# Two transformer blocks with 64 experts on one core: other first experts, bias tables without GpSimd, a shorter seam, shared products split

## The chip, the cores and the metric

The kernel runs on one core of a Trainium2 chip. The metric is the device time of one execution in microseconds; three executions of the kernel before were timed. A fourth was taken by the hardware profiler, and every row below is from that one. TensorE (PE) multiplies; VectorE (DVE), ScalarE (ACT) and GpSimd (POOL) work elementwise; SyncE (SP) issues nearly all DMAs, each in the order of its queue.

## The reference

The input is one sequence of 256 tokens, 1024 wide. The first block has two layers. Each adds a mixture of three branches (windowed attention with a bias by relative position, a convolution over 31 positions, latent attention) and a feed-forward of 4096. After a final norm the second block modulates the rows with a vector, runs retention and a gated delta rule, and then 64 experts: each token goes to 8 of them, out of 4 of 8 groups, beside one expert that all tokens share. Everything is float32.

```python
def swa_bias_and_mask(positions, rel_bias):
    ...
    bucket = t5_bucket(pq[..., :, None] - pk[..., None, :])
    bias = rel_bias[bucket].astype(jnp.float32).reshape(b, nb, WINDOW, 2 * WINDOW, SWA_KV_HEADS, SWA_GROUP)
...
def first_block(x, positions, rel_bias, g_final, ...):
    swa_bias, swa_mask = swa_bias_and_mask(positions, rel_bias)
    for l in range(DEPTH):
        h = rms_norm(x, g_mix[l])
        q_a, k_a, v_a, u_b, cq_c, ckv_c, kpe_c, gate_logits = jnp.split(h @ w_in[l], IN_SPLIT_POINTS, axis=-1)
        y_a = swa_attention(q_a, k_a, v_a, swa_sinks[l], swa_bias, swa_mask)
        y_b = conformer_conv(u_b, w_dw[l], b_dw[l], g_conv_ln[l], b_conv_ln[l])
        y_c = mla_attention(cq_c, ckv_c, kpe_c, positions, ...)
        branches = jnp.einsum('bsnc,ncd->bsnd', jnp.stack([y_a, y_b, y_c], axis=2), w_branch[l])
        gates = jax.nn.sigmoid(gate_logits.reshape(b, s, N_BRANCHES, D_MODEL))
        x = x + jnp.einsum('bsnd,bsnd->bsd', gates, branches) @ w_out[l]
        h = rms_norm(x, g_mlp[l])
        x = x + jnp.square(jax.nn.relu(h @ w_up[l])) @ w_down[l]
    return rms_norm(x, g_final)
...
def _moe(h, w_router_l, bias_l, w_gate_l, w_up_l, w_down_l, w_sh_gate_l, w_sh_up_l, w_sh_down_l):
    scores = jax.nn.sigmoid((xt @ w_router_l).astype(jnp.float32))
    ...
    sel = lax.top_k(cand, TOP_K)[1]
    wts = jnp.take_along_axis(scores, sel, axis=1)
    wts = wts / jnp.sum(wts, axis=-1, keepdims=True) * ROUTED_SCALE
    ...
        return (jax.nn.silu(xe @ w_gate_l[e]) * (xe @ w_up_l[e])) @ w_down_l[e]
    ...
    shared = (jax.nn.silu(xt @ w_sh_gate_l) * (xt @ w_sh_up_l)) @ w_sh_down_l
    return (routed + shared).reshape(b, l, d)
```

## The kernel before

Activations lie transposed, model dimension on partitions, 256 tokens along the free axis. Dense weights are read as 128 x 1024 tiles of 512 KB (`raw`, line 323). ScalarE rounds each to a high part `whi`, VectorE (some GpSimd) subtracts it and keeps the low part `wlo`; a dense product is three products of 256 tokens, X high and low with `whi` and X high with `wlo`. `Kern.run` goes through layer 0 (`mix`, `ff`), layer 1, the final norm, the mixers of the second block (`mixer2`) and the experts (`moe`). Except for the experts' part, a scheduler sets each engine's order.

*Bias tables.* `t5_bias` (line 423) builds `self.bias`, the position bias of both windows for eight heads, in layer 0. Six times GpSimd subtracts positions of 16 keys from those of 128 queries into `n` (int32, 128 x 2048, two buffers), VectorE compares `n` with a threshold on each partition into `oh` (bf16, two buffers), TensorE multiplies `oh` with three parts of the bias differences, and VectorE adds the mask, head by head: 48 additions of 128 x 64. Queries, keys, values and the convolution's gate `gt` are projected at the same time; their `wlo` splits are in the same VectorE queue.

*Seam.* The last feed-forward's output comes in pairs of tiles: `bt` is the product scaled, `xT` the sum with the residual. `add_sq` (line 506) squares each tile on ScalarE (`sq`, once plain, once with the final gain) and sums them on GpSimd (`sqacc`). `final_norm` (line 1346) sums over partitions on TensorE, takes an inverse root on VectorE (`rsqrt`, line 470), spreads it over all partitions (`rows`, line 489), and then does the same for the norm that follows in the second block; `modulated` (line 928) makes the eight tiles of the input `X` with it, and `final_x` (beside it in the queue) the normed residual `xT`.

*Experts.* Weights of this stage go through `ring` (line 1618), 25 slots of 512 KB in which a tile is loaded once and read as it is. SP issues them in the order of the code. The shared expert has four tiles `w_sh` and two `w_shd`; each expert six, four `w_gu` (gate and up) and two `w_ed` (down). Experts are sorted by their number of tokens on the device. The tables `TIERS` give the positions in that order (first position, token slots for each expert), and `ORDER` the sequence of groups; a group has 256 slots and two units of 128 slots, so a unit holds one, two or four experts. The first `PRE` of the sorted experts are fixed, 0, 1 and 2 here, whatever their counts: their tiles are issued without knowing the routing. For the others SP loads the expert's number (`ids`) first, and so waits for the router. 

```python
NRING = 25
PRE = 3
TIERS = ((0, 128), (8, 64), (32, 32))
ORDER = (0, 2, 0, 1, 1, 2, 0, 1, 1, 2, 0, 1, 1, 2)
...
        j = U["js"][i]
        if j < PRE:
            return slice(j, j + 1)
        if i not in U["reg"]:
            U["reg"][i] = self.nc.values_load(self.ids[0:1, j:j + 1], engines=[mybir.EngineType.SP], ...
```

With these tables the first group holds experts 0 and 1, 128 slots each. `shared` (line 1771) multiplies all four `w_sh` tiles ahead of the experts (`st` is its activation, `hs` its hidden rows). `experts` (line 1834) writes TensorE's order by hand: `gather` makes a one-hot matrix `oh` on VectorE and copies the group's tokens with products `pm<-oh,tok` into `xg`; a unit then has `gate_up` (line 1888, `pd<-ring,xg`), the next group's gathering, and `down` (`pm<-ring,hT`). `overflow` (line 1973) is a branch on the device: if any expert has more tokens than its tier has slots (counts against the tiers, `fl`), it reads the experts again.

## Time and profile before

| | us |
|---|---|
| median of three executions | 1885.78 (1885.19 to 1888.55) |
| profiled execution, whole | 1888.56 |
| its span | 1886.8 |
| PE busy | 1769.1 (94%) |
| DVE busy | 1203.6 (64%) |
| ACT busy | 780.9 (41%) |
| POOL busy | 212.5 (11%) |
| bytes by DMA | 414.45 MB, 220 GB/s over the span |

The busy time of an engine is an average over stages that differ. The first block lasts to about 1050 us, the mixers to about 1340, the experts to the end. In the last row, the mean of 220 GB/s stands for slices of 81 to 251 GB/s up to about 1415 us and of 406 to 409 behind that, but for the last.

### The profile page before, as it was taken

Reading aid. Unit: us, or ns where it says so; the run is one execution under the profiler, and the core shown is the slowest. Engines: PE = TensorE matmul, PEld = TensorE weight load, DVE = VectorE, ACT = ScalarE, POOL = GpSimd, SP = SyncE. Lnnn points to the kernel's source line nnn. Section 1 sums busy time; section 2 is a strip of 40 time slices with the busy share of each in tenths; the row PEclk is TensorE's granted clock in tenths of the full one; section 3 lists DMA queues with packets and bytes.
Section 4 is the critical chain, followed back from the end, with each engine's and each line's share of the span. In section 5 each row is a group of like instructions: output and inputs, shape, how many; then the busy total and the mean of one; then the engine's idle time right before and its main releaser. Section 6 shows DMA issues by size and latency. Waiting matters only on the chain.

```text
span 1886.8 us, 37800 instructions
## 1 busy us (share of the span) xinstructions
PE 1769.1 (94%) x15105; PEld 1462.3 (78%) x15105; DVE 1203.6 (64%) x2383; ACT 780.9 (41%) x1409; POOL 212.5 (11%) x158
## 2 busy tenths in 40 slices
PE   5988999999999999999999899899999999999996
PEld 5987999999997899999889798799854443443441
DVE  7989887988798687866857688458622332332323
ACT  4247655444447655555354445444322121221211
POOL 3344200000053502000002000000100000000000
PEclk9889999999999999999989899999899999999999
DMA  4334555777542456756545342334579999999996
GB/s 158 118 101 127 176 168 178 251 240 247 170 138 81 158 168 201 225 172 199 160 146 178 95 145 81 110 102 131 211 250 398 408 408 409 409 409 409 408 406 237
DMA packets 122146, 414.45 MB, mean 220 GB/s; under 512 B 13937, under 2 KB 14833, under 8 KB 121969
## 3 DMA queue, kind: packets, MB, share of 16 engines
q1 hardware_dynamic: 120528, 409.92, 61.9%
q8 instruction: 119, 1.95, 0.4%
q10 hardware_dynamic: 1440, 2.11, 0.4%
q14 instruction: 59, 0.48, 0.1%
HBM read 410.92 MB, written 1.05 MB: 218 GB/s over the span
## 4 chain that ended last, share of the span: by engine, by line
PE 51%; DMA 13%; DVE 4%; issue 3%; ACT 2%; POOL 2%; SPq 0%; POOLq 0%; DVEq 0%; ACTq 0%
PE pd L290 36%; PE pm L290 14%; DMA ring<-in_w_gu 8%; DMA ring<-in_w_ed 4%; POOL wlo L302 1%; PE pst L290 1%; PE pm L966 1%; POOL sqacc L302 1%; DVE wlo L302 1%; DVE iY L302 0%; ACT iZ L299 0%; ACT whi L299 0%; ACT E L299 0%; PE pm L1926 0%; DVE pst L311 0%
## 5 line engine op out<-in xcount | busy, mean ns | idle before, releaser
L290 PE MATMUL pd<-X,whi 128*128 128x256 f32 (+1 forms) x3280 | 635.8, 294 | 11.9 <-ACT whi L299 8.3
L299 ACT ACTIVATE whi<-raw 128x1024 fp32r<-128x1024 f32 x340 | 356.8, 1052 | 504.2 <-PE pd L290 393.1
L290 PEld LDWEIGHTS pd<-X,whi 128*128 128x128 f32 (+1 forms) x3280 | 532.6, 198 | 17.0 <-ACT whi L299 8.5
L290 PE MATMUL pd<-X,wlo 128*128 128x256 f32 (+1 forms) x1640 | 481.0, 294 | 15.3 <-DVE wlo L302 12.1
L302 DVE TENSOR_TENSOR wlo<-raw,whi 128x1024 fp32r<-128x1024 f32 x286 | 352.9, 1238 | 115.2 <-ACT whi L299 114.1
L290 PEld LDWEIGHTS pd<-X,wlo 128*128 128x128 f32 (+1 forms) x1640 | 324.7, 198 | 19.9 <-DVE wlo L302 13.4
L290 PE MATMUL pd<-ring,xg 128*32 128x512 f32 (+2 forms) x1024 | 235.2, 596 | 10.0 <-DMA ring<-in_w_gu 9.9
L290 PEld LDWEIGHTS pd<-ring,xg 128*32 128x32 f32 (+2 forms) x1024 | 71.6, 130 | 168.6 <-issue 108.8
L290 PE MATMUL pd<-H,whi 128*128 128x256 f32 x1024 | 185.5, 283 | 0.0
L290 PEld LDWEIGHTS pd<-H,whi 128*128 128x128 f32 x1024 | 157.6, 189 | 0.5
L311 DVE SCALAR_TENSOR_TENSOR tg<-tg,pd 128x256 f32<-128x256 f32 x28 | 11.8, 421 | 219.4 <-ACT tg L299 219.4
L302 POOL TENSOR_TENSOR wlo<-raw,whi 128x1024 fp32r<-128x1024 f32 (+1 forms) x54 | 127.5, 2373 | 170.4 <-ACT whi L299 155.2
L290 PE MATMUL pd<-H,wlo 128*128 128x256 f32 x512 | 143.9, 281 | 0.0
L311 DVE SCALAR_TENSOR_TENSOR pst<-up,vec,pst 128x256 f32<-128x256 f32 x240 | 116.4, 485 | 3.7
L290 PE MATMUL pm<-ring,hT 128*32 128x512 f32 (+2 forms) x512 | 111.4, 598 | 2.7 <-DMA ring<-in_w_ed 1.7
L299 ACT ACTIVATE tg<-pd 128x256 f32<-128x256 f32 x28 | 10.8, 384 | 235.4 <-PE pd L290 235.4
L311 DVE SCALAR_TENSOR_TENSOR acc<-rawm,sl,acc 128x512 f32<-128x512 f32 x112 | 87.6, 794 | 20.8 <-DMA rawm<-in_w_mod 20.3
L290 PEld LDWEIGHTS pd<-H,wlo 128*128 128x128 f32 x512 | 96.5, 189 | 0.0
L302 DVE TENSOR_TENSOR y<-pm,y 128x512 fp32r<-128x512 f32 x56 | 38.5, 691 | 86.8 <-ACT y L299 86.8
L302 POOL TENSOR_TENSOR sqacc<-sqacc,sq 128x256 f32<-128x256 f32 x42 | 37.3, 897 | 488.4 <-ACT sq L299 487.2
L299 ACT ACTIVATE y<-pm 128x512 fp32r<-128x512 f32 (+1 forms) x58 | 34.4, 597 | 121.8 <-PE pm L290 121.8
L290 PEld LDWEIGHTS pm<-ring,hT 128*32 128x32 f32 (+2 forms) x512 | 33.3, 129 | 65.9 <-issue 52.4
(532 smaller groups left out, 2645.0 us busy)
## 6 DMA issues: line engine op xcount, KB each, us to landing
ring<-in_w_gu SPq DMA_DIRECT2D x256, 512.0 KB, 10.1
ring<-in_w_ed SPq DMA_DIRECT2D x128, 512.0 KB, 10.1
raw<-in_w_up SPq DMA_DIRECT2D x64, 512.0 KB, 4.2
raw<-in_w_dn SPq DMA_DIRECT2D x64, 512.0 KB, 4.2
raw<-in_w_g SPq DMA_DIRECT2D x48, 512.0 KB, 3.7
rawm<-in_w_mod SPq DMA_DIRECT2D x96, 256.0 KB, 3.4
raw<-in_w_s SPq DMA_DIRECT2D x32, 512.0 KB, 3.6
raw<-in_w_x SPq DMA_DIRECT2D x32, 512.0 KB, 3.6
```

The lines of the kernel that those rows point to most:

```text
L290: return self.nc.tensor.matmul(out, l, r, start=start, stop=stop)
L299: self.nc.scalar.activation(out, in_, f, **kw)
L302: return (eng or self.nc.vector).tensor_tensor(out, a, b, op)
L311: self.nc.vector.scalar_tensor_tensor(out, a, s, b, op0, op1)
L966: self.nc.tensor.transpose(ps[:, i * P:(i + 1) * P], x, self.ident)
```

## The change

Four edits. (1) Four experts instead of three are fixed, and the tables put them alone into the first group, 64 slots each, two to a unit. The next eight have 128 slots, twenty have 64, the rest 32; there are still 14 groups, 28 units and 384 tiles of experts. The first group's one-hot is made with priority, and the flags of `overflow` follow the new tiers. (2) `t5_bias` compares positions as f32 on VectorE, with no GpSimd subtraction, and adds the mask for eight heads at once. (3) At the seam the squares of the last two tiles are summed on TensorE directly (`last_sums`), both roots are taken together in four columns (`args` gives `rsqrt` its argument), and `r12`, with the tiles `X`, comes ahead of `r1` and `xT`. (4) `shared` multiplies two of its four tiles ahead of the experts and one behind each of the first two units' gate and up products; `st` has one buffer.

```diff
@@ -41,7 +41,7 @@
-PRE = 3
+PRE = 4
@@ -51,9 +51,9 @@
 SHD = 2
-TIERS = ((0, 128), (8, 64), (32, 32))
-
-ORDER = (0, 2, 0, 1, 1, 2, 0, 1, 1, 2, 0, 1, 1, 2)
+TIERS = ((0, 64), (4, 128), (12, 64), (32, 32))
+
+ORDER = (0, 3, 1, 2, 2, 3, 1, 2, 2, 3, 1, 2, 1, 3)
@@ -428,6 +428,12 @@
+        qf = tp.tile([P, S], F32, name="qf")
+        nc.vector.tensor_copy(qf, self.pq)
+        kf = tp.tile([P, 96], F32, name="kf")
+        nc.vector.tensor_copy(kf, pk)
+        self.ts(kf, kf, th, ALU.add)
@@ -449,12 +455,9 @@
             for h0 in range(0, nk, 16):
-                n = tp.tile([P, 16, P], I32, name="n", bufs=2)
-                self.tt(n, self.pq[:, None, b * P:(b + 1) * P].to_broadcast([P, 16, P]),
-                        pk[:, b * 32 + h0:b * 32 + h0 + 16][:, :, None].to_broadcast([P, 16, P]),
-                        ALU.subtract, nc.gpsimd)
                 oh = tp.tile([P, 16, P], BF16, name="oh", bufs=2)
-                self.ts(oh, n, th, ALU.is_ge)
+                self.tt(oh, qf[:, None, b * P:(b + 1) * P].to_broadcast([P, 16, P]),
+                        kf[:, b * 32 + h0:b * 32 + h0 + 16][:, :, None].to_broadcast([P, 16, P]), ALU.is_ge)
@@ -463,18 +466,20 @@
                 mk = self.c("mca" if b == 0 else "mband").rearrange("p (g k) -> p g k", g=4)[:, :, h0:h0 + 16]
-                for h in range(8):
-                    self.tt(dst[:, h], src[:, h], mk, ALU.add)
-
-    def rsqrt(self, src, n, scale, eps, ps=None):
+                self.tt(dst, src, mk[:, None].to_broadcast([P, 8, 4, 16]), ALU.add)
+
+    def rsqrt(self, src, n, scale=None, eps=None, ps=None):
...
         f = (2.0 * (8.0 / 3) ** 3) ** 2
-        self.ts(v, src, scale * f, ALU.mult, eps * f, ALU.add)
+        if callable(src):
+            src(v, f)
+        else:
+            self.ts(v, src, scale * f, ALU.mult, eps * f, ALU.add)
@@ -643,6 +648,23 @@
+            def last_sums(k):
+
+                if k == KD - 2:
+                    ps = res["sums"] = self.pst_()
+                    parts = [(i, a) for i, a in enumerate(res["acc"])]
+                else:
+                    ps, parts = res["sums"], []
+                for i in range(2):
+                    sq = self.ap.tile([P, S], F32, name="sq", tag="sq", bufs=2)
+                    self.act(sq, self.xT[:, k], AF.Square, **({"scale": self.v("g_final", None, k)} if i else {}))
+                    parts.append((i, sq))
+                for n, (i, x) in enumerate(parts):
+                    for t in range(2):
+                        c = i * 2 + t
+                        self.mm(ps[:, c:c + 1], x[:, t * P:(t + 1) * P], self.ones[:, 0:1], k == KD - 2 and n + t == 0,
+                                k == KD - 1 and i + t == 2)
@@ -650,7 +672,9 @@
                 for k in (f, f + 1):
-                    if last:
+                    if last and f == KD - 2:
+                        last_sums(k)
+                    elif last:
@@ -925,10 +949,10 @@
-    def modulated(self, x, r, a, b, X, pool):
+    def modulated(self, x, r, a, b, X, pool, tag="cvy", bufs=2):
         for k in range(KD):
-            t = pool.tile([P, 2, S], F32, name="mt", tag="cvy", bufs=2)[:, 0]
+            t = pool.tile([P, 2 * S if tag == "cvy" else S], F32, name="mt", tag=tag, bufs=bufs)[:, 0:S]
@@ -1343,24 +1367,25 @@
-    def final_norm(self, accs):
-
-        x = self.xT
-        c1, r1 = self.rstd([accs[0]], D, "rf1")
+    def final_norm(self, ps):
...
         self.ga = ga
-        ps = self.pst_()
-        for t in range(2):
-            self.mm(ps[:, t:t + 1], accs[1][:, t * P:(t + 1) * P], self.ones[:, 0:1], True, True)
-        v = self.sp.tile([P, 2], F32, name="v2", tag="v2")
-        self.tt(v, c1, c1, ALU.mult)
-        self.tt(v, v, ps[:, 0:2], ALU.mult)
+        w = self.sp.tile([P, 2], F32, name="v2", tag="v2")
+
+        def args(v, f):
+
+            self.ts(w, ps[:, 2:4], f / D, ALU.mult)
+            self.ts(v[:, 0:2], ps[:, 0:2], f / D, ALU.mult, f * EPS, ALU.add)
+            self.stt(v[:, 2:4], v[:, 0:2], EPS, w, ALU.mult, ALU.add)
+        with self.tc.high_priority():
+            c = self.rsqrt(args, 4, ps=ps[:, 256:304])
+            r12 = self.rows(c[:, 2:4], self.ap.tile([P, S], F32, name="r12", tag="rf2"))
+        r1 = self.rows(c[:, 0:2], self.ap.tile([P, S], F32, name="rf1", tag="rstd", bufs=4))
         self.sxx = self.sp.tile([P, 2], F32, name="sxx")
-        self.nc.vector.tensor_copy(self.sxx, v)
-        c2 = self.rsqrt(v, 2, 1.0 / D, EPS)
-        self.tt(v, c1, c2, ALU.mult)
-        r12 = self.rows(v, self.ap.tile([P, S], F32, name="r12", tag="rf2"))
+        self.tt(w, c[:, 0:2], c[:, 0:2], ALU.mult)
+        self.tt(self.sxx, w, ps[:, 2:4], ALU.mult)
@@ -1381,7 +1406,8 @@
             with tp("mr") as rp, tp("m1") as pool:
-                self.modulated([x[:, k] for k in range(KD)], r12, self.ga, self.x_b, X, pool)
+                with tc.high_priority():
+                    self.modulated([x[:, k] for k in range(KD)], r12, self.ga, self.x_b, X, pool, "mt", 4)
@@ -1608,10 +1634,10 @@
                 self.tokens(X)
-                down = self.shared(X, a)
+                rest, down = self.shared(X, a)
...
                 self.mb = b
-                self.experts(down)
+                self.experts(rest, down)
@@ -1717,7 +1743,7 @@
         fl = rt.tile([1, 8], F32, name="fl")
-        at = [(j, 128) for j in range(PRE + 1)] + [t for t in TIERS[1:]]
+        at = [(j, TIERS[0][1]) for j in range(PRE)] + [t for t in TIERS[1:]]
@@ -1770,14 +1796,17 @@
+        self.mb = pool
...
         def cb(f, ps, nf):
-            t = pool.tile([P, S], F32, name="st", tag="st", bufs=2)
+            t = self.mb.tile([P, S], F32, name="st", tag="st", bufs=1)
...
             self.stt(hs[:, f // 2], t, 0.5, ps[:, S:2 * S], ALU.mult, ALU.mult)
-        self.dense(lambda i: self.A["w_sh"][i], KD, 4, X, cb)
+        dense = self.dense_g(lambda i: self.A["w_sh"][i], KD, 4, X, cb)
+        for _ in range(2):
+            next(dense)
@@ -1786,7 +1815,7 @@
                 self.add_out(t, hf, ps)
-        return [lambda hf=hf: down(hf) for hf in range(2)]
+        return [lambda: next(dense)] * 2, [lambda hf=hf: down(hf) for hf in range(2)]
@@ -1831,7 +1860,7 @@
-    def experts(self, first):
+    def experts(self, rest, first):
@@ -1839,8 +1868,10 @@
         with self.tc.manual_schedule(engines={mybir.EngineType.PE}):
-            st, steps = self.gather(*groups[0])
-            for f in steps:
+            with self.tc.high_priority():
+                st, steps = self.gather(*groups[0])
+                steps[0]()
+            for f in steps[1:]:
@@ -1865,6 +1896,8 @@
                 self.hidden(U)
+                if i < len(rest):
+                    rest[i]()
@@ -2085,7 +2118,7 @@
                     self.dump_states()
-                    r1, r12 = self.final_norm(res["acc"])
+                    r1, r12 = self.final_norm(res["sums"])
```

The order of three places follows, each before and then after, read from the built programs.

VectorE at the tables. `bias` is the mask addition, `oh` the compare, `wlo` the split of a weight tile for the projections, `gt` the convolution's gate. Before, from the second half of the tables on:

```order
L302 TENSOR_TENSOR bias_385<-pm,cstm 128x4x16 x16
L307 TENSOR_SCALAR oh<-n,cst 128x2048 x2
L302 TENSOR_TENSOR wlo<-raw,whi 128x1024
L302 TENSOR_TENSOR bias_386<-pm,cstm 128x4x16 x16
L307 TENSOR_SCALAR oh<-n,cst 128x2048 x2
L302 TENSOR_TENSOR wlo<-raw,whi 128x1024
L302 TENSOR_TENSOR bias_386<-pm,cstm 128x4x16 x16
L302 TENSOR_TENSOR gt<-pd,r_156 128x256 x2
```

After:

```order
L302 TENSOR_TENSOR bias_386<-pm,cstm 128x32x16
L302 TENSOR_TENSOR oh<-qf,kf 128x2048
L302 TENSOR_TENSOR bias_386<-pm,cstm 128x32x16
L302 TENSOR_TENSOR oh<-qf,kf 128x2048
L302 TENSOR_TENSOR bias_386<-pm,cstm 128x32x16
L302 TENSOR_TENSOR wlo<-raw,whi 128x1024
L302 TENSOR_TENSOR bias_386<-pm,cstm 128x32x16
L302 TENSOR_TENSOR gt<-pd,r_156 128x256 x2
```

The compares now stand between single additions instead of ahead of lots of 16; `gt` still follows the last addition.

VectorE at the seam, from the last step of the first root. `sm` and `pst` hold the roots' columns, `v` a root. Before:

```order
L302 TENSOR_TENSOR v_12720<-sm 128x2
L302 TENSOR_TENSOR v_12720<-v_12720,pst 128x2
L1360 COPY sxx<-v_12720 128x2
L308 TENSOR_SCALAR sm<-v_12720 128x2
L307 TENSOR_SCALAR sm<-sm 128x2
L308 TENSOR_SCALAR sm<-sm 128x2
L302 TENSOR_TENSOR sm<-sm 128x2 x2
L311 SCALAR_TENSOR_TENSOR sm<-sm 128x2 x2
L302 TENSOR_TENSOR sm<-sm 128x2 x2
L311 SCALAR_TENSOR_TENSOR sm<-sm 128x2
L302 TENSOR_TENSOR v_12720<-sm 128x2
L311 SCALAR_TENSOR_TENSOR mt<-xT,ga,r_12737 128x256 x2
```

After, from the last steps of the one root (`pst` and `sm` with four columns):

```order
L311 SCALAR_TENSOR_TENSOR sm<-pst,sm 128x4
L302 TENSOR_TENSOR pst<-pst,sm 128x4 x2
L311 SCALAR_TENSOR_TENSOR sm<-pst,sm 128x4
L302 TENSOR_TENSOR v_12658<-sm 128x2
L302 TENSOR_TENSOR sxx<-v_12658,pst 128x2
L311 SCALAR_TENSOR_TENSOR mt<-xT,ga,r_12672 128x256 x3
L311 SCALAR_TENSOR_TENSOR X<-mt,mod,X 128x256 x3
L311 SCALAR_TENSOR_TENSOR mt<-xT,ga,r_12672 128x256 x3
L311 SCALAR_TENSOR_TENSOR X<-mt,mod,X 128x256 x3
L311 SCALAR_TENSOR_TENSOR mt<-xT,ga,r_12672 128x256 x2
L311 SCALAR_TENSOR_TENSOR xT<-xT,vec,rf_12677 128x256
L311 SCALAR_TENSOR_TENSOR X<-mt,mod,X 128x256 x2
```

The second root is gone, and `xT` stands behind the `X` tiles rather than between them.

SP's queue at the start of the experts, after the last dense weights (`w_o`); the ISA row belongs to a load at a register's address. Before:

```order
L323 DMA raw<-in_w_o 128x1024 x8
L1621 DMA ring<-in_w_sh 128x1024 x4
L1621 DMA ring<-in_w_gu 128x1024 x4
L1621 DMA ring<-in_w_ed 128x1024 x2
L1621 DMA ring<-in_w_gu 128x1024 x4
L1621 DMA ring<-in_w_ed 128x1024 x2
L1827 TENSOR_LOAD ids
L1621 ISA
L1621 DMA ring<-in_w_gu 128x1024
```

After:

```order
L323 DMA raw<-in_w_o 128x1024 x8
L1647 DMA ring<-in_w_sh 128x1024 x2
L1647 DMA ring<-in_w_gu 128x1024 x8
L1647 DMA ring<-in_w_sh 128x1024
L1647 DMA ring<-in_w_ed 128x1024 x4
L1647 DMA ring<-in_w_gu 128x1024 x8
L1647 DMA ring<-in_w_sh 128x1024
L1647 DMA ring<-in_w_ed 128x1024 x4
L1856 TENSOR_LOAD ids
L1647 ISA
L1647 DMA ring<-in_w_gu 128x1024
```

Ahead of the first expert number there are 28 tiles instead of 16. Since the ring has 25 slots, the last three of the 28 wait for TensorE to free slots.

## Rows read from the trace of the kernel before

**Rows 1.** The page, part 4, the chain that ended last, by engine and line

```profile
...
PE pd L290 36%; PE pm L290 14%; DMA ring<-in_w_gu 8%; DMA ring<-in_w_ed 4%; POOL wlo L302 1%; PE pst L290 1%; PE pm L966 1%; POOL sqacc L302 1%; DVE wlo L302 1%; DVE iY L302 0%; ACT iZ L299 0%; ACT whi L299 0%; ACT E L299 0%; PE pm L1926 0%; DVE pst L311 0%
...
```

**Rows 2.** Windows of start and expert stage: length, then busy us, PEclk, DMA share, GB/s

```profile
...
40.00:60.00 20.00, 13.90 (x214) 13.30 (x213) 18.97 (x48) 3.56 (x4) 6.33 (x2) 0.74 0.26 79
80.00:100.00 20.00, 16.12 (x135) 15.73 (x133) 19.46 (x31) 5.86 (x8) 13.32 (x6) 1.00 0.55 172
1340.00:1360.00 20.00, 15.66 (x103) 14.29 (x101) 15.41 (x90) 8.30 (x20) 0.00 (x0) 0.83 0.04 13
1360.00:1380.00 20.00, 18.19 (x105) 15.49 (x104) 7.92 (x28) 6.40 (x14) 0.00 (x0) 1.00 0.89 333
1380.00:1400.00 20.00, 19.53 (x80) 10.64 (x80) 4.39 (x11) 5.14 (x10) 0.00 (x0) 1.00 0.54 173
1400.00:1420.00 20.00, 19.53 (x139) 9.98 (x138) 6.57 (x20) 5.53 (x11) 0.00 (x0) 1.00 0.74 249
1440.00:1540.00 100.00, 99.79 (x483) 49.17 (x482) 32.12 (x68) 22.30 (x42) 0.00 (x0) 1.00 1.03 409
...
```

**Rows 3.** Timeline of POOL, 16 to 82: start, length, engine, line, operation, count [idle before]

```profile
...
16.63 7.22 POOL L302 TENSOR_TENSOR n<-pq,pk 128x2048 int32<-128x2048 int32 x2 [15.66 <-DMA pk<-in_pos_k]
...
79.94 2.41 POOL L302 TENSOR_TENSOR wlo<-raw,whi 128x1024 fp32r<-128x1024 f32 x1 [9.42 <-DVE gt L302]
```

**Rows 4.** Timeline of DVE, 16 to 75

```profile
...
16.71 3.68 DVE L307 TENSOR_SCALAR ang<-ang,cst 128x256 f32<-128x256 f32 x1
...
32.14 0.34 DVE L308 TENSOR_SCALAR ang<-ang,cst 128x256 f32<-128x256 f32 x1
...
41.32 4.00 DVE L443 COPY w<-part 32x8 bf16<-32x8 bf16 x4
...
45.41 1.22 DVE L302 TENSOR_TENSOR wlo<-raw,whi 128x1024 fp32r<-128x1024 f32 x1
...
47.76 0.68 DVE L443 COPY w<-part 32x8 bf16<-32x8 bf16 x4
...
53.61 2.42 DVE L302 TENSOR_TENSOR bias<-pm,cstm 128x64 f32<-128x64 f32 x16 [0.61 <-PE pm L290]
55.95 2.47 DVE L307 TENSOR_SCALAR oh<-n,cst 128x2048 bf16<-128x2048 int32 x2
58.33 4.63 DVE L302 TENSOR_TENSOR wlo<-raw,whi 128x1024 fp32r<-128x1024 f32 x1
...
```

**Rows 5.** Waits of PE, 20 to 80: us in total, times, longest

```profile
...
PE pd L290 <- DVE wlo L302: 10.6, 2, 5.4
PE pm L290 <- DVE oh L307: 2.2, 1, 2.2
...
```

**Rows 6.** Timeline of all engines at the seam, 1035.5 to 1051.5

```profile
...
1036.09 0.69 DVE L302 TENSOR_TENSOR bt<-pd,rm 128x512 f32<-128x512 f32 x1 [1.44 <-PE pd L290]
...
1037.60 0.42 ACT L299 ACTIVATE sq<-xT 128x256 f32<-128x256 f32 x1 [0.57 <-DVE xT L302]
...
1038.10 3.17 POOL L302 TENSOR_TENSOR sqacc<-sqacc,sq 128x256 f32<-128x256 f32 x4 [11.29 <-ACT sq L299]
...
1040.64 1.01 PE L290 MATMUL pst<-ones,sqacc 128*128 128x1 f32 x4 [4.59 <-POOL sqacc L302]
...
1047.91 0.16 DVE L302 TENSOR_TENSOR v<-sm 128x2 f32<-128x2 f32 x1
...
1050.88 0.79 PE L290 MATMUL pd<-X,whi 128*128 128x256 f32 x2 [1.53 <-ACT X L299]
...
```

**Rows 7.** Timelines of SP's queue and of PE as the experts begin, 1315 to 1412

```profile
...
1361.03 26.59 SPq L1621 DMA_DIRECT2D ring<-in_w_gu  x16
...
1364.98 10.53 PE L290 MATMUL pd<-y,ring 128*128 128x256 f32 x48
1377.32 4.23 PE L290 MATMUL pm<-oh,tok 128*128 128x256 f32 x32 [1.81 <-DVE oh L302]
...
1381.86 7.11 PE L290 MATMUL pd<-ring,xg 128*128 128x512 f32 x16
...
```

## Prediction

> **What bounds the kernel now.** I read the chain of work that ended last first, because it says which resources set the end: TensorE's products take half of it, and the only transfers with a share worth naming are the 512 KB tiles of the experts, 12% together [rows 1]. So until the experts begin, time is won only where TensorE waits, and in the expert stage it may also be won at the DMA. The stretches say when. From 1440 us on the DMA moves 409 GB/s without a pause; between 1340 and 1420 it does not [rows 2]. Missing against 409 GB/s are 19.4 us of the 20 from 1340 to 1360, 3.7 to 1380, 11.5 to 1400 and 7.8 to 1420, together **42.4 us**. TensorE is busy in the same stretches, and I return to that in the rivals. Two earlier places remain: the bias tables and the seam between the two blocks. In each I read the engines' timeline, and for the first also the waits of TensorE.
>
> **Part 1, bias tables (16 to 80 us).** Removed are six int32 subtractions on GpSimd, the first two of which last 7.22 us [rows 3]. What they cost is not their own time: VectorE instructions that start beside one end when it ends. One `ang` takes 3.68 us beside the first pair and another of the same shape 0.34 later; four `w` copies take 4.00 and, alone, 0.68; a `wlo` takes 4.63 and, alone, 1.22 [rows 4]. Two more rows lose 3.2 and 3.4 us in the same way and a pair of `oh` 1.3, so VectorE loses 3.3 + 3.3 + 3.4 + 3.2 + 3.4 + 1.3 = 18 us. Added: the six compares become instructions with two f32 inputs of 2048 elements. No row has that form at that size. The nearest is `wlo`, 1.22 us for 1024 [rows 4], so at most 2.44; an `oh` now takes 1.24 (2.47 for two), so the six cost 6 x 1.2 = 7 us more. Forty-eight small additions (2.42 us for 16, 2.18 for the other two lots) become six of 512 elements, 0.69 each by `bt` [rows 4, 6]: 2.6 us less. The two casts and one addition cost about 0.6. VectorE comes out 18 - 7 + 2.6 - 0.6 = 13 us ahead. TensorE waits here for VectorE 10.6 + 2.2 = 12.8 us [rows 5], and after such waits its granted clock averages 0.74 from 40 to 60, which is the lower of its two levels (1.2 GHz) for about half of that stretch [rows 2]. So it has that much to gain. I take **-11 us**: the 13 less something that the work behind it, for which VectorE is busy 19.5 of 20 us [rows 2], gives back. Bounds: -6 if half comes back, -15 if the faster clock adds to it. If the long VectorE rows have another cause, nothing is won and the 7 - 2.6 + 0.6 = 5 us are lost.
>
> The Trainium skill, "SBUF — State Buffer", section "Who interferes with whom", says that a VectorE instruction with two inputs in SBUF shuts out, or is shut out by, a GpSimd instruction that reads SBUF, for the whole of it. That agrees with the 4.63 us `wlo`, and it speaks against the change, since the new compares have two such inputs. By that rule six meetings with a GpSimd instruction of 2.41 us would cost up to 14.5 us and leave nothing of part 1; by the rows as they stand it is worth the -11. In the new order GpSimd issues nothing but memsets ahead of the `wlo` split that now starts at 79.94 [rows 3], so none of the six is met.
>
> **Part 2, the seam (1036 to 1051 us).** Now the four squares of the last two tiles go through GpSimd (3.17 us), TensorE sums them at 1040.64, VectorE makes one inverse root, a second sum follows, then a second root until 1048.07, and the first product of the second block starts at 1050.88 [rows 6]. In the changed kernel ScalarE's four squares run one after the other from 1037.60, at about 0.4 us each to 1039.3, TensorE adds them with the earlier partial sums by 1040.1, one root of twelve steps at the present pitch of 0.2 us ends at 1042.5, and the way from there to the first product stays what it is, 1050.88 - 1048.07 = 2.8 us: 1045.3, which is 5.5 earlier. Four `xT` updates that stand between the eight `X` tiles now move behind them, 0.48 us each on VectorE, of which about 1 us is on the path. **-6 us**; bounds -4 (the 16 sums on TensorE, 0.25 us each as in the 1.01 us row, all in the way) and -8. What is late next is VectorE's `X` tiles.
>
> **Part 3, the experts.** Both kernels bring 390 tiles of 0.524 MB, 1.28 us each at 409 GB/s, 499 us of transfer, so the end moves by what the pause shrinks. *Before:* four tiles of the shared expert and twelve of two known experts go out, the last of them has landed near 1340.6 (13 GB/s from 1340 to 1360 is half a tile [rows 2]), and SyncE waits for the routed expert numbers until 1361.03 [rows 7]. After that it waits for free slots, because a first group of two experts frees 12 tiles in two units. *After:* four known experts make 24 tiles; the ring has 25 slots, so 25 tiles can go out ahead of any free slot instead of 16 ahead of the numbers. Nine more keep the DMA busy for 9 x 1.28 = 11.5 us longer, to about 1352. The first slots come free when the first half of the shared products ends. All of them run in 10.53 us in their main stretch [rows 7], 0.44 for each of 24 pairs; sixteen of the 32 pairs move behind units 0 and 1, 7.0 us. So the gathering, now 1377.32, begins at 1370.3 and unit 0's products at 1374.9 instead of 1381.9. Units 0 and 1 each free twelve tiles rather than six, and last 3.5 us longer for their eight moved pairs. Idle DMA time is then about 13 us (1352 to 1365), 8 of the 11 to 1376, and 2 to 7 in restarts: 22 to 28 instead of 42.4, a gain of 14 to 20. I take **-14 us**, the low end, because a tile issued into an empty queue still needs its flight before TensorE can use it and each of the refills waits for a slot to be freed. Bounds: -9 (a pause of 33) and -20. The moved products cost nothing on TensorE as long as the DMA sets the pace, which it does after 1440 [rows 2]; without that cover they are the same 7 us, later. The `onehot` of the first group has priority in the new order, but on VectorE it still stands behind the shared expert's `st` and `hs`; I count nothing for it.
>
> **Sum.** -11 - 6 - 14 = -31. The profiled execution took 1888.56 us, with 1.8 around its span of 1886.8; that gives 1857.6. It is 2.8 above the median of the three runs, 1885.78, so against the median I say **1855 us**.
>
> **Rivals.**
> 1. *The bias gain is given back.* VectorE and TensorE are both busy behind the tables, 19.5 and 16.1 of 20 us from 80 to 100 [rows 2], and the new order moves the convolution later among the attention's work there. For it: what ends the stretch is work that needs both, and a saved wait can reappear at the convolution's end. Against: VectorE, 19 of 20 us busy [rows 2], has 13 us less to do. Price: part 1 is 0 to -3, the time 1863 to 1866.
> 2. *TensorE, not the DMA, sets the expert stage.* It shows 99.8 of 100 us busy from 1440 to 1540 [rows 2]; then an earlier DMA is worth little beyond the earlier first unit, part 3 is -2 to -4 and the time 1865 to 1867. Against: the chain holds 12% of expert transfers [rows 1].
> 3. *The whole pause closes.* With twelve tiles freed by each of the first two units the ring never runs dry; part 3 is -20 and part 1 -13, the time 1846 to 1849.
> 4. *Slower: the overflow branch.* The known experts' limit falls from 128 tokens to 64, and the next eight get 128, the next twenty 64, the rest 32. If one count is over its limit the device takes the branch that reads experts again; all 384 tiles at 1.28 us would be 490 us, a time near 2345. It decides as soon as one known expert has 65 tokens. From the reference's inputs the four have 13, 16, 29 and 11, and none of the sorted others passes its tier, so only a rounding far larger than the margins would bring it.
> 5. *The change does not do what it says:* the compares still meet GpSimd, or the nine further tiles wait for a slot or for the numbers all the same. The new order excludes the first and shows such a wait only from the 26th tile on.
>
> **How the numbers follow.** Chances: my forecast 0.60, rival 1 0.14, rival 2 0.12, rival 3 0.10, rivals 4 and 5 with other mishaps 0.04. The bounds added up straight would be -19 and -43; all three at one end together is unlikely, so the forecast's own range is 1848 to 1862. To hold eight in ten I reach to rival 3 on one side and to rivals 1 and 2 on the other: 1844 to 1867. What can be told from no change here is about 0.2%, 3.8 us, which is far inside every case but the fourth and a sum of mishaps: faster 0.95, same 0.02, slower 0.03.
>
> **What would show it.** Part 1: no VectorE row of 3 to 4 us between 16 and 70, compares of at most 2.44 us, `gt` about 11 us earlier, TensorE's waits for `wlo` nearly gone. That the convolution ends as much earlier as `gt` speaks for the forecast, an unchanged end for rival 1. Part 2: first product of the second block about 9.3 us after `bt` rather than 14.8. Part 3: DMA at full rate to about 1352 less the 17 us won before it, a pause of 22 to 28 us in place of 42, unit 0 about 7 us earlier against the routing. The prediction is wrong if the long `wlo` rows stay without GpSimd, if a pause as long as 42 us remains, or if TensorE's waits for ring tiles vanish while the time of the stage stays.

## The result, and the profile after

The changed kernel takes 1863.62 us in the median (1860.42 to 1865.47, four runs), the kernel before beside it 1885.67 (1885.19 to 1888.55, four runs): ratio **0.9878**, 95% interval 0.9862 to 0.9893, so 20 to 26 us less. I had forecast 1855 with a range of 1844 to 1867: right in direction, inside the range, 9 us too optimistic. The profiled executions took 1888.56 and 1862.92 us; the first is the slowest of its four runs, so the traces differ by 25.6 us where the medians differ by 22.0. Trace lengths below are to be read with that.

The same steps of the program can be laid beside one another:

| step | before, us | after, us | earlier by |
|---|---|---|---|
| `gt`, first | 71.88 | 57.41 | 14.5 |
| first `w_uq` issued | 113.8 | 89.4 | 24.4 |
| first `w_out` issued | 252.2 | 237.9 | 14.3 |
| first product of the feed-forward, `pd<-H,whi` | 339.8 | 325.7 | 14.1 |
| last `bt` of the first block | 1036.09 | 1020.68 | 15.4 |
| first product of the second block | 1050.88 | 1030.88 | 20.0 |
| first product of unit 0 | 1381.9 | 1354.0 | 27.9 |
| last product of the experts | 1870.9 | 1844.5 | 26.4 |

The bias tables gave a lead of 24 us, of which 10 went back between 200 and 240. The seam gave 4.6. Unit 0 starts 7.9 us earlier still, and of that the end has only 6.4 left: 26.4 - 20.0.

**Bias tables.** VectorE's timeline answers to [rows 4]:

```profile
...
25.29 2.28 DVE L302 TENSOR_TENSOR oh<-qf,kf 128x2048 bf16<-128x2048 f32 x1
...
35.64 0.68 DVE L449 COPY w<-part 32x8 bf16<-32x8 bf16 x4
...
36.43 1.22 DVE L302 TENSOR_TENSOR wlo<-raw,whi 128x1024 fp32r<-128x1024 f32 x1
...
57.41 0.75 DVE L302 TENSOR_TENSOR gt<-pd,r 128x256 f32<-128x256 f32 x2
...
61.75 3.11 DVE L302 TENSOR_TENSOR wlo<-raw,whi 128x1024 fp32r<-128x1024 f32 x1
...
```

A `wlo` takes 1.22 us and four `w` copies 0.68 with nothing on GpSimd; no row of 3 to 4 us is left ahead of 60 us. One stands behind it, so my sign "between 16 and 70" held only to 60: the `wlo` at 61.75 lasts 3.11 us, beside a `wlo` split of GpSimd itself, which now starts at 61.38 and takes 2.40. The change took the subtractions away and left these meetings. The compare takes 2.28 us, not the 2.44 of my bound, and the last one ends at 54.4, ahead of GpSimd's splits. TensorE's waits from 20 to 80 us, against [rows 5]:

```profile
...
PE pd L290 <- DVE wlo L302: 1.3, 2, 1.0
...
```

10.6 us became 1.3, and the clock of 40 to 60 went from 0.74 to 1.00. From `gt` to the first `w_uq` the lead grows from 14.5 to 24.4 us: in this stretch (72 to 114 before, 57 to 90 after) TensorE's clock is 1.00 rather than 0.91, and a wait of 4.3 us for `sqc` is gone; how much each of the two gave was not measured. Then the gain shrinks. The windows (as in [rows 2]) and the waits of TensorE from 190 to 260:

```profile
...
40.00:60.00 20.00, 19.65 (x386) 19.27 (x384) 18.27 (x22) 5.89 (x7) 0.20 (x1) 1.00 0.36 117
...
200.00:220.00 20.00, 12.56 (x80) 11.52 (x78) 13.87 (x33) 7.19 (x12) 0.00 (x0) 0.80 0.44 130
220.00:240.00 20.00, 17.91 (x138) 17.91 (x139) 13.46 (x22) 10.01 (x18) 0.00 (x0) 0.86 0.30 92
...
```

```profile
...
PE pd L290 <- ACT yb L299: 3.5, 1, 3.5
PE pm L290 <- ACT cv L299: 2.6, 1, 2.6
PE pm L290 <- DVE sm L311: 2.0, 1, 2.0
PE pst L290 <- ACT up L299: 1.4, 1, 1.4
...
```

TensorE is busy 12.56 of 20 us from 200 to 220, at a clock of 0.80, and waits 3.5 + 2.6 + 2.0 + 1.4 = 9.5 us on the chain of the convolution's norm (`cv`, `sm`, `up`, `yb`). The groups of DMA issues (duration min/median/max in ns, first and last start) and of products show the lead on both sides of that:

```profile
...
L323 SPq DMA_DIRECT2D raw<-in_w_out x16: 327/328/328, 237.9 to 693.7; - x16
...
L323 SPq DMA_DIRECT2D raw<-in_w_uq x4: 327/328/328, 89.4 to 538.2; - x4
...
```

```profile
...
L290 PE MATMUL pd<-H,whi x1024: 276/281/582, 325.7 to 1020.2; 128*128 128x256 f32 x171
...
```

The products of the experts are grouped in the same way, gate and up first, down behind:

```profile
...
L290 PE MATMUL pd<-ring,xg x1024: 592/592/697, 1354.0 to 1834.3; 128*32 128x512 f32 x84, 128*64 128x512 f32 x63, 128*128 128x512 f32 x24
L290 PE MATMUL pm<-ring,hT x512: 592/592/697, 1367.9 to 1844.5; 128*32 128x512 f32 x84, 128*64 128x512 f32 x63, 128*128 128x512 f32 x24
...
```

**Seam.** All engines, against [rows 6]:

```profile
...
1020.68 0.69 DVE L302 TENSOR_TENSOR bt<-pd,rm 128x512 f32<-128x512 f32 x1 [1.45 <-PE pd L290]
...
1022.66 2.75 PE L290 MATMUL pst<-ones,sq 128*128 128x1 f32 x16 [1.23 <-ACT sq L299]
1023.36 0.42 ACT L299 ACTIVATE sq<-xT 128x256 f32<-128x256 f32 x1 [0.36 <-PE pst L290]
...
1025.45 0.16 DVE L307 TENSOR_SCALAR v<-pst 128x2 f32<-128x2 f32 x1 [2.22 <-PE pst L290]
...
1027.66 0.16 DVE L311 SCALAR_TENSOR_TENSOR sm<-pst,sm 128x4 f32<-128x4 f32 x1
...
1030.88 1.10 PE L290 MATMUL pd<-X,whi 128*128 128x256 f32 x3 [0.87 <-ACT X L299]
...
```

From `bt` to the first product it takes 10.20 us instead of 14.79. The sums are ready 4.77 us after `bt` starts, where I had 4.0: the second tile's squares wait 0.36 us for TensorE, which still reads the two `sq` buffers. From the end of the root to the first product it is 3.06 us.

**Experts.** The windows after, against [rows 2]:

```profile
...
1320.00:1340.00 20.00, 15.62 (x110) 13.79 (x108) 16.11 (x99) 8.77 (x22) 0.00 (x0) 0.91 0.70 280
1340.00:1360.00 20.00, 18.19 (x113) 12.41 (x114) 7.83 (x24) 6.99 (x14) 0.00 (x0) 1.00 0.30 95
1360.00:1380.00 20.00, 19.53 (x104) 10.46 (x101) 4.34 (x11) 4.06 (x8) 0.00 (x0) 1.00 0.97 354
1380.00:1400.00 20.00, 19.53 (x153) 10.73 (x152) 6.42 (x20) 5.95 (x12) 0.00 (x0) 1.00 1.02 384
...
1720.00:1780.00 60.00, 60.00 (x280) 30.87 (x278) 19.18 (x40) 13.68 (x26) 0.00 (x0) 1.00 1.02 405
1780.00:1800.00 20.00, 19.56 (x102) 12.59 (x100) 5.13 (x14) 4.84 (x10) 0.00 (x0) 1.00 0.93 339
1800.00:1820.00 20.00, 17.31 (x104) 7.95 (x108) 7.26 (x18) 3.32 (x7) 0.00 (x0) 0.91 0.71 248
...
```

Missing against 409 GB/s are 6.3 us of the first 20, then 15.4, 2.7 and 1.2: a pause of **25.6 us**, in the 22 to 28 that I forecast. But there is a second one that the kernel before does not have: 3.4 us from 1780 to 1800 and 7.9 from 1800 to 1820, **11.3 us**. Ahead of it TensorE is busy 60.00 of 60 us. The chain of work that ended last, in order of time (start, length, what, count), and the waits of SP's queue from 1770 to 1825 (total, times, longest) say what happens there:

```profile
...
1789.90 6.87 PE pd L290 x16
1812.32 10.38 DMA ring<-in_w_gu
...
```

```profile
...
SPq L1647 <- PE pm L290: 12.1, 7, 7.0
SPq L1647 <- PE pd L290: 6.6, 7, 1.2
...
```

From 1711 to 1811 the chain runs through products, and only the three transfers from 1812 on are on it again. SP waits 12.1 + 6.6 us for products to free slots, up to 7.0 us at once.

### The profile page after: what moved, and what is told of

Same layout as the page of the kernel before. It is cut to its first block, busy times and chain, and to the rows that moved or that the text cites. A ratio compares the mean times of both kernels' runs of the same rounds, so it can differ in the third digit from the quotient of the medians.

```text
span 1860.8 us, 37772 instructions
## 1 busy us (share of the span) xinstructions
PE 1757.5 (94%) x15121; PEld 1452.7 (78%) x15121; DVE 1185.9 (64%) x2335; ACT 781.8 (42%) x1409; POOL 185.0 (10%) x148
## 4 chain that ended last, share of the span: by engine, by line
PE 51%; DMA 12%; DVE 5%; issue 3%; ACT 2%; POOL 1%; SPq 0%; POOLq 0%; DVEq 0%; ACTq 0%
PE pd L290 36%; PE pm L290 14%; DMA ring<-in_w_gu 7%; DMA ring<-in_w_ed 4%; POOL wlo L302 1%; PE pst L290 1%; PE pm L990 1%; DVE wlo L302 1%; DVE iY L302 0%; DVE pst L311 0%; DMA cT<-in_ctxT 0%; ACT iZ L299 0%; ACT E L299 0%; ACT whi L299 0%; POOL sqacc L302 0%
## 5 line engine op out<-in xcount | busy, mean ns | idle before, releaser
L290 PE MATMUL pd<-X,whi 128*128 128x256 f32 (+1 forms) x3280 | 626.6, 291 | 11.5 <-ACT whi L299 8.0
L290 PEld LDWEIGHTS pd<-X,whi 128*128 128x128 f32 (+1 forms) x3280 | 524.5, 195 | 16.3 <-ACT whi L299 8.0
L290 PE MATMUL pd<-X,wlo 128*128 128x256 f32 (+1 forms) x1640 | 476.2, 291 | 5.8 <-POOL wlo L302 3.3
L290 PEld LDWEIGHTS pd<-X,wlo 128*128 128x128 f32 (+1 forms) x1640 | 319.8, 195 | 10.2 <-POOL wlo L302 4.5
L290 PE MATMUL pd<-ring,xg 128*32 128x512 f32 (+2 forms) x1024 | 231.0, 595 | 8.4 <-DMA ring<-in_w_gu 8.4
L302 POOL TENSOR_TENSOR sqacc<-sqacc,sq 128x256 f32<-128x256 f32 x38 | 33.4, 887 | 490.5 <-ACT sq L299 489.3
```

The costliest lines, as they stand in the source:

```text
L290: return self.nc.tensor.matmul(out, l, r, start=start, stop=stop)
L302: return (eng or self.nc.vector).tensor_tensor(out, a, b, op)
```

## The experiments

Each ran beside the kernel before on the same chip, in three sets; the changed kernel was not run again in them. The medians of the kernel before are 1885.67 us in the run of the result and 1887.05, 1888.85 and 1887.63 in the three sets, and single runs of one kernel differ by up to 12 us (`u_seam` 1866.4 to 1878.4). So a difference to the changed kernel, whose ratio is 0.9862 to 0.9893, is clear only where the intervals of the ratios lie apart, and differences of 2 us are read in the traces alone. In the traces I compare the last product of the experts with the last product of the mixers' input: 530.9 us lie between them in the kernel before, 524.3 in the changed one.

### One part undone at a time

`u_bias` puts the function for the tables back:

```diff
-                self.tt(oh, qf[...], kf[...], ALU.is_ge)
+                self.tt(n, self.pq[...], pk[...], ALU.subtract, nc.gpsimd)
+                oh = tp.tile([P, 16, P], BF16, name="oh", bufs=2)
+                self.ts(oh, n, th, ALU.is_ge)
...
-                self.tt(dst, src, mk[:, None].to_broadcast([P, 8, 4, 16]), ALU.add)
+                for h in range(8):
+                    self.tt(dst[:, h], src[:, h], mk, ALU.add)
```

> The bias tables are made as in the kernel before, the rest is the changed kernel. Theory: part 1 is a shift of everything behind it and is worth what the milestones show, 14 us (first product of layer 0's feed-forward 339.8 before, 325.7 after), so the time is about 1877 to 1878 us, ratio to before 0.996. Rival: the lead at 340 us is partly due to the other edits' reordering, or the later stages give it back; then the time is 1868 to 1872. In the trace VectorE rows of 3 to 4.6 us beside GpSimd's subtractions are back.

Measured: 1877.2 us, ratio 0.9941 (0.9918 to 0.9964). That is 13.6 above the changed kernel, as the theory has it (by the ratios about 12, with the intervals apart). `gt` stands at 71.88 again and the feed-forward at 339.7. The run undoes subtractions, compares and additions together and prices none of them apart.

`u_seam` puts back the sums on GpSimd and the two roots, and `xT` between the `X` tiles:

```diff
-                    if last and f == KD - 2:
-                        last_sums(k)
-                    elif last:
+                    if last:
...
-                    r1, r12 = self.final_norm(res["sums"])
+                    r1, r12 = self.final_norm(res["acc"])
```

> The seam is made as in the kernel before, the rest is the changed kernel. Theory: the seam is worth the 4.6 us by which the way from bt to the first product of the second block became shorter (14.8 to 10.2 us), so the time is 1867 to 1869 us. Rival: my forecast of 6, with the X tiles behind it, 1869 to 1871; or the expert stage gives it back, 1864.

Measured: 1867.38 us, ratio 0.9911 (0.9882 to 0.994), 3.8 above. The interval overlaps that of the changed kernel, so the times can't tell the 4.6 of the trace from my 6. The trace can: from `bt` at 1018.42 to the first product at 1033.22 it takes 14.80 us again.

`u_moe` puts back the tables, the shared expert and the gathering:

```diff
-PRE = 4
+PRE = 3
-TIERS = ((0, 64), (4, 128), (12, 64), (32, 32))
-ORDER = (0, 3, 1, 2, 2, 3, 1, 2, 2, 3, 1, 2, 1, 3)
+TIERS = ((0, 128), (8, 64), (32, 32))
+ORDER = (0, 2, 0, 1, 1, 2, 0, 1, 1, 2, 0, 1, 1, 2)
...
-                if i < len(rest):
-                    rest[i]()
```

> Tables, known experts, shared expert and gathering as in the kernel before, bias tables and seam of the changed kernel. Theory: the expert part is worth only 6 to 7 us net, because the pause of the DMA at its start shrank by 17 us but a new one of 11 us stands at 1781 to 1821; so the time is 1869 to 1871 us. Rival: the late pause has nothing to do with the edit (it comes from being earlier); then it is in this run too and the time is about 1877 to 1880. No late pause is expected by the theory: 406 GB/s or more up to the last tiles.

Measured: 1872.22 us, ratio 0.9921 (0.9894 to 0.9948), 8.6 above and 1.2 over the theory's upper end. Its windows show no late pause, though its routing comes within 5 us of the changed kernel's:

```profile
...
1780.00:1800.00 20.00, 20.00 (x120) 11.18 (x116) 4.47 (x11) 4.15 (x8) 0.00 (x0) 1.00 1.02 406
1800.00:1820.00 20.00, 16.88 (x119) 7.56 (x119) 7.47 (x20) 4.03 (x8) 0.00 (x0) 0.93 1.02 405
...
```

So the pause belongs to the changed expert part and not to the hour; which piece of that part brings it, `x_order` shows below. `u_shared` undoes the split of the shared expert alone:

```diff
-        for _ in range(2):
-            next(dense)
+        self.dense(lambda i: self.A["w_sh"][i], KD, 4, X, cb)
...
-                if i < len(rest):
-                    rest[i]()
```

> The changed kernel with the shared expert's four tiles all multiplied ahead, as before. Theory: the first products of unit 0 come 7 us later against the routing (40.7 instead of 33.7 us after the last product of the mixers' input), the first pause is 4 to 7 us longer and the late pause shorter by nearly as much, so edit 4 is worth 0 to 3 us by itself: 1864 to 1867 us. Rival (only the first pause counts): 1868 to 1871.

Measured: 1865.54 us, ratio 0.9894 (0.9869 to 0.9919), 1.9 above: by itself the split is worth little, within the 0 to 3 us of the theory, and its interval reaches to nothing. Unit 0 starts at 1362.8, 41.9 us after the last product of the mixers' input as in the kernel before. Of the theory's mechanism one half came: the first pause is 29.4 us, 3.8 longer (269, 106 and 250 GB/s in the slices from 1320 to 1380), but the late pause is not shorter, 11.0 us (362 and 232 GB/s from 1780 to 1820). The last product is 1.5 us later against the mixers' input; why only that, stays open.

### GpSimd beside VectorE

`b_pool` is the changed kernel with the subtractions added, whose result nobody reads:

```diff
+                n = tp.tile([P, 16, P], I32, name="n", bufs=2)
+                self.tt(n, self.pq[...], pk[...], ALU.subtract, nc.gpsimd)
                 oh = tp.tile([P, 16, P], BF16, name="oh", bufs=2)
```

> The changed kernel with the six int32 subtractions back on GpSimd, but nobody reads them and nobody waits for them. Theory (the two engines exclude each other for whole instructions): VectorE rows that start beside a subtraction last until it ends, 2 to 4 us longer, compares among them; VectorE loses 10 to 20 us before 60 us and the time is 1869 to 1880. Rival (the cost was VectorE waiting for n, and GpSimd for free buffers): the VectorE rows keep their usual lengths and the time is 1863 to 1865.

Measured: 1886.44 us (ten runs), ratio 1.0002 (0.9989 to 1.0016): the whole gain of all four edits is gone. GpSimd's row, and VectorE's rows beside and behind it:

```profile
...
16.73 21.98 POOL L302 TENSOR_TENSOR n<-pq,pk 128x2048 int32<-128x2048 int32 x6 [15.77 <-DMA pk<-in_pos_k]
...
```

```profile
...
16.99 3.58 DVE L308 TENSOR_SCALAR rk<-ang,cst 128x256 f32<-128x256 f32 x1
...
31.48 3.57 DVE L311 SCALAR_TENSOR_TENSOR pst<-sm 128x2 f32<-128x2 f32 x1
...
39.44 1.21 DVE L302 TENSOR_TENSOR wlo<-raw,whi 128x1024 fp32r<-128x1024 f32 x1
...
45.47 2.29 DVE L302 TENSOR_TENSOR oh<-qf,kf 128x2048 bf16<-128x2048 f32 x1
...
```

Six subtractions run back to back until 38.7, and six VectorE instructions last until one of them ends: 3.58 us for 128 x 256, and 3.57 us for one of only 128 x 2, whose usual length is 0.16. Behind 39 us every form has its usual length again. Nobody waits for `n`, so this is not the handshake: VectorE is held up by what GpSimd runs beside it. The compares start later than the last subtraction here, so none of them met one, against the expectation. The time is above the 1869 to 1880 that I expected, a loss of 23 us: all six came early, with nothing between them, and TensorE waited for the `wlo` behind them, 19.1 us at one time (waits from 20 to 90 us):

```profile
...
PE pd L290 <- DVE wlo L302: 20.3, 2, 19.1
...
```

The kernel before shows two things more, in rows beside those of [rows 3] and [rows 4], first GpSimd, then VectorE:

```profile
...
57.30 9.13 POOL L302 TENSOR_TENSOR n<-pq,pk 128x2048 int32<-128x2048 int32 x2 [12.19 <-DVE oh L307]
...
62.89 2.18 DVE L302 TENSOR_TENSOR bias<-pm,cstm 128x64 f32<-128x64 f32 x16
...
```

GpSimd is held up as well: these two subtractions take 9.13 us where the first two took 7.22. And not every instruction of VectorE is: the sixteen mask additions from 62.89 on, with one input in PSUM (`pm`) and one in SBUF, take 2.18 us beside the subtraction that runs until 66.4, the same as the sixteen from 69.78 on with no subtraction beside them.

The Trainium skill, "SBUF — State Buffer", section "Who interferes with whom", calls this an exclusive lock for a whole instruction; the 128 x 2 row with 3.57 us agrees with that.

### What took back ten microseconds in layer 0

`x_conv` leaves ten of 31 taps of layer 0's convolution out:

```diff
-                    for t in range(1, 31):
+                    for t in range(1, 31 if l else 21):
```

> The changed kernel without the last 10 of the 31 taps of layer 0's convolution (40 VectorE instructions of 0.485 us, 19 us, left out; layer 1 keeps all). Theory: the lead of layer 0 falls from 24 us (at 107 to 177) to 14 (at 238), because the convolution on VectorE ends only 9 us earlier than before and TensorE then waits for what follows it; with 19 us of it gone TensorE's waits of 200 to 240 us vanish and the feed-forward starts 8 to 10 us earlier (first product at 316 to 318 instead of 325.7), the time 1854 to 1856. Rival (ScalarE or the order of the gates' products set that end): the feed-forward starts at most 3 us earlier, the time 1861 to 1864.

Measured: 1855.27 us, ratio 0.9832 (0.9809 to 0.9855), 8.4 below the changed kernel, and the feed-forward starts at 316.7 instead of 325.7. The windows:

```profile
...
200.00:220.00 20.00, 20.00 (x169) 20.00 (x170) 16.63 (x34) 12.59 (x22) 0.00 (x0) 1.00 0.45 140
220.00:240.00 20.00, 20.00 (x171) 20.00 (x170) 15.93 (x20) 8.59 (x9) 0.00 (x0) 1.00 0.65 197
...
```

TensorE is busy 20.00 of 20 us and its waits are gone (0.4 us of 9.9 from 190 to 260). With the tables out of the way the convolution on VectorE (120 taps of 0.48 us in a layer) ends the stretch. Its last tap ends at 218.4 in the kernel before and at 207.4 in the changed one, 11.0 us earlier, where `gt` is 14.5 earlier.

### The late pause

`x_order` changes the sequence of the groups alone:

```diff
-ORDER = (0, 3, 1, 2, 2, 3, 1, 2, 2, 3, 1, 2, 1, 3)
+ORDER = (0, 3, 1, 2, 1, 3, 2, 1, 2, 3, 1, 2, 2, 3)
```

> The changed kernel with another sequence of the same groups: the two groups of 128 slots with one of 64 between them stand ahead of the second group of 32 slots instead of ahead of the last. Theory (the ring fills while TensorE works on experts of 128 slots, 12 tiles in 30 us): the pause of 11 us leaves 1781 to 1821 and appears near 1490 to 1540, the last 300 us run at 405 GB/s or more, and the time stays within 2 us of 1863.6. Rival (something at the end of the kernel slows the transfers, the final rows for one): the pause stays where it is.

Measured: 1865.28 us, ratio 0.9893 (0.9858 to 0.9929). The pause moved with the two groups of 128 slots: 1.1 + 8.0 us from 1500 to 1540, and 408 GB/s where it was.

```profile
...
1500.00:1520.00 20.00, 20.00 (x70) 10.77 (x70) 5.20 (x10) 4.23 (x8) 0.00 (x0) 1.00 0.99 387
1520.00:1540.00 20.00, 20.00 (x145) 10.82 (x144) 7.69 (x21) 5.39 (x11) 0.00 (x0) 1.00 0.73 245
...
1740.00:1820.00 80.00, 76.40 (x460) 35.16 (x456) 22.25 (x52) 15.02 (x29) 0.00 (x0) 1.00 1.03 408
...
```

That excludes a cause at the end of the kernel. A group of 128 slots is 12 tiles, and TensorE needs 30 us for it, in which the DMA can bring 23; two of them ahead of the next group of 32 slots are more lead than 25 slots hold.

`x_units` gives each unit its own tier, so that a group may hold one expert with 128 slots and four with 32. `gather` builds the one-hot matrix in two pieces where the halves differ:

```diff
-ORDER = (0, 3, 1, 2, 2, 3, 1, 2, 2, 3, 1, 2, 1, 3)
+ORDER = (0, 0, 3, 3, 1, 3, 2, 2, 1, 3, 2, 2, 1, 3, 1, 2, 1, 3, 2, 2, 1, 3, 2, 2, 1, 2, 1, 3)
...
-            groups.append((tiers[i].pop(0), 256 // TIERS[i][1]))
+        halves = [(tiers[i].pop(0), 128 // TIERS[i][1]) for i in ORDER]
+        groups = list(zip(halves[0::2], halves[1::2]))
```

> The changed kernel, but a group may pair two units of different tiers, so that a unit of one expert with 128 slots (6 tiles) is followed by one of four with 32 (24 tiles); the units and tiles are the same. Theory: the ring never fills behind 1400 us, the late pause of 11 us is gone, 400 GB/s or more up to the last tile, and the time is 1852 to 1854 us. Rival (TensorE sets the stage, the DMA's lead is worth nothing): 1861 to 1865.

Measured: 1860.29 us, ratio 0.9856 (0.9827 to 0.9884). The theory missed: the late pause is gone, as said, but the time is only 3 us lower, 0.7 below the rival's 1861 to 1865 and not clear of the changed kernel. The last product comes 522.3 us after that of the mixers' input, 2.0 earlier. The windows at the end, the group of the down products (first and last start), and the last products on the chain of work that ended last:

```profile
...
1760.00:1820.00 60.00, 59.76 (x276) 29.99 (x274) 16.66 (x35) 12.66 (x24) 0.00 (x0) 1.00 1.02 406
1820.00:1835.00 15.00, 12.67 (x73) 6.00 (x76) 3.49 (x10) 0.77 (x2) 0.00 (x0) 0.89 0.85 339
...
```

```profile
...
L290 PE MATMUL pm<-ring,hT x512: 592/592/644, 1371.4 to 1844.5; 128*32 128x512 f32 x87, 128*64 128x512 f32 x65, 128*128 128x512 f32 x19
...
```

```profile
...
1839.63 7.51 PE pm L290 x48
...
```

The DMA is busy 0.85 of the last 15 us, so its full rate ends near 1832; the last product starts 12 us later, at 1844.5, and no transfer is on the chain behind 1755. The lead that the units of 128 slots build up is a debt if they stand at the end: TensorE must still work it off. `x_end` therefore lets the sequence end with two units of 32 slots:

```diff
-ORDER = (0, 0, 3, 3, 1, 3, 2, 2, 1, 3, 2, 2, 1, 3, 1, 2, 1, 3, 2, 2, 1, 3, 2, 2, 1, 2, 1, 3)
+ORDER = (0, 0, 3, 3, 1, 2, 1, 3, 2, 2, 1, 2, 1, 3, 1, 2, 1, 3, 2, 2, 1, 2, 1, 3, 2, 2, 3, 3)
```

> Mixed pairs of units as in x_units, but in a sequence that ends with two units of 32 slots and has no pair of 128-slot units without a 32-slot unit behind. Theory: in x_units the last tile landed 10 us earlier against the routing, but TensorE was 11 us behind the transfers at the end, because the units ahead of the last were of 128 slots; ending with two units of 32 slots TensorE has caught up when the last tile lands (some 4 us to the last product, as in the changed kernel), so the last product comes 514 to 516 us after the last product of the mixers' input (changed kernel 524.2, x_units 522.2) and the time is 1853 to 1856 us. Rival: TensorE as a whole is too slow; then the last product stays at 520 or later and the time at 1859 to 1862.

Measured: **1855.36 us**, ratio 0.984 (0.982 to 0.9861), below both kernels, though its interval only just lies apart from the changed kernel's. The same views:

```profile
...
1760.00:1820.00 60.00, 52.90 (x268) 17.84 (x270) 10.33 (x25) 5.61 (x11) 0.00 (x0) 0.97 1.02 408
1820.00:1835.00 15.00, 12.29 (x57) 3.58 (x58) 4.46 (x8) 2.45 (x5) 0.00 (x0) 1.00 0.69 276
...
```

```profile
...
L290 PE MATMUL pm<-ring,hT x512: 592/592/1063, 1369.0 to 1837.2; 128*32 128x512 f32 x86, 128*64 128x512 f32 x65, 128*128 128x512 f32 x20
...
```

```profile
...
1825.10 10.76 DMA ring<-in_w_ed
1835.90 3.98 PE pm L290 x18
...
```

There is no late pause. The DMA's full rate ends near 1830, against the mixers' input within 1 us of `x_units`; the last tile lands at 1835.9, the last products follow at once, and the last of them starts at 1837.2. That is 516.5 us after the last product of the mixers' input, 0.5 above the forecast's upper end and 5.8 less than in `x_units`. This difference in the traces shows the debt; the medians of the two, 1860.29 and 1855.36, have intervals that overlap.

The other three multiply one shared tile ahead and three behind:

```diff
-        for _ in range(2):
-            next(dense)
+        next(dense)
...
+        return {1: 1, 2: 2}, lambda: next(dense), [...]
```

> The changed kernel with one of the four shared tiles multiplied ahead and three behind (one at unit 1, two at unit 2). Theory: unit 0 starts about 5 us earlier against the routing and the first pause shrinks by 3 to 5, but the late pause grows by as much, since the ring holds no more; the time stays within 2 us of 1863.6. Rival (the first pause alone sets the time): 1858 to 1860.

> Both edits together: mixed pairs of units and one shared tile ahead, three behind. Theory: with no late pause to swallow it the earlier start counts, 1847 to 1850 us. Rival (the two don't add): 1852 to 1854 as with mixed pairs alone.

> x_end with one shared tile multiplied ahead and three behind. Theory: the first pause gets 2 to 4 us shorter and nothing behind it takes that back: 1850 to 1853 us. Rival: no better than x_end.

Measured: `x_one` 1859.52 us (0.9847, 0.9813 to 0.9881), `x_best` 1860.25 (0.9862, 0.9836 to 0.9888), `x_end1` 1854.62 (0.9829, 0.9808 to 0.9851). The theories of `x_one` and `x_best` missed, and of `x_best` the rival too; that of `x_end1` came in the first pause, about 2 us shorter, and not in the time, 1.6 above its range. In `x_one` unit 0 starts only 0.9 us earlier against the mixers' end, not 5. VectorE's casts for the routing weights are as late as before; the one-hot stands right behind them, so that the gathering starts 2.5 us earlier, but TensorE, which had waited 2.8 us for it, ran it at a granted clock of 0.70 and took 5.69 us instead of 4.15 at 1.00. The first pause got 1.6 us shorter, not 3 to 5, and the late pause did not grow (10.4 us against 11.3). In the times `x_best` is `x_units` again and `x_end1` is `x_end` again within their intervals. In the traces the last product comes earlier against the mixers' input each time: 520.6 us in `x_one` for 524.3 in the changed kernel, 519.6 in `x_best` for 522.3, 514.9 in `x_end1` for 516.5. One trace of each is not enough to call the further split, worth 1.6 to 3.7 us by these, shown.

## Why the prediction was right, and where it was not

- *Part 1, forecast -11, measured -14.1 in the trace and 13.6 by undoing it.* The mechanism holds: that GpSimd's subtractions hold VectorE up is shown by `b_pool` and not only argued. VectorE came out 14.5 ahead at `gt` rather than 13, the compares being shorter than the bound. "Something that the work behind it" gives back was right in kind, and both of its sizes were off: the lead grew to 24 us, with TensorE at its full clock and one wait less, and the convolution's end took 10 back. That the two misses leave 14 beside my 11 is in part luck. It is rival 1 in part, and `x_conv` shows its place: the convolution ended 11.0 us earlier, neither as much as `gt` nor unchanged.
- *Part 2, forecast -6, measured -4.6 and 3.8.* Mis-sized: "sums by 1040.1" was 0.8 too early, the way to the first product 0.3 too short, and the microsecond for the moved `xT` is not there (the last product with X is 19.8 us earlier, the first 20.0).
- *Part 3, forecast -14, measured -6.4 and 8.6.* The terms were right, and the conclusion was not. Unit 0 came 7.9 us earlier (7.0 forecast), the first pause fell from 42 us to 25.6 (22 to 28 forecast). What failed is "the end moves by what the pause shrinks": I took the DMA as busy to the end once it was busy. The lead it had gained filled the ring, and 11.3 us of it were lost to a second pause. `x_order` moves that pause, `u_moe` has none, `x_units` and `x_end` avoid it. Rival 2, that TensorE sets the stage, was true for a part of it, and I had put it as all or nothing: without the late pause `x_units` gains only 2 us, until `x_end` lets TensorE catch up.
- *Sum.* -14.1 - 1.3 (between 340 and 1036, in no step of the change) - 4.6 - 6.4 = -26.4 at the last product, 25.6 for the whole of the profiled executions. Against medians it is 22, since the profiled run of before is 2.9 above its median and that of the changed kernel 0.7 below. Part 1 came out 3 us better than forecast and so hides a part of the 7.6 us that part 3 lacks.
- The overflow branch is not taken, as the time shows, and rivals 3 and 5 did not come; of rival 3's reason, that the ring never runs dry, the opposite decided: late in the stage it was full.

## What to carry to other kernels

A queue of prefetched tiles has two ends: ask not only how long the transfers stand still at the start, but where the buffers fill when the consumer's need per tile changes, and sequence the stages so that slow consumers never stand together and the fast ones stand last. An idle engine's work is not free if it shares something with the busy one: look for rows of one engine that end when a row of another ends. And when a wait goes, write down what is late next with its time, for here it took back ten of 24 us.

## What was not expected

An instruction of VectorE with 128 x 2 elements took 3.57 us beside GpSimd, more than twenty times its usual 0.16; the loss goes by the number of instructions that meet, not by their size, and sixteen additions with an input in PSUM lost nothing beside the same engine. And ten runs with the six unread subtractions are as slow as the kernel before, 1886.44 against 1887.05 us.
